# Layer-norm sums through a constant block, four instead of eight units on the un-normed residual, and a reordered last norm

## The chip, the cores and the metric

The kernel runs on one core of a Trainium2 chip. The metric is device time in microseconds (us). The core has a TensorE (in the profile PE for its matmuls and PEld for its weight loads), a VectorE (DVE), a ScalarE (ACT), a GpSimd (POOL) and a SyncE (SP, which here issues nearly all DMAs). Each engine works through its own instruction queue in the order in which the program puts instructions there, and waits on semaphores for the others.

## The reference

A two-layer decoder trunk over 256 tokens with 2048 channels, all float32. Each layer is a mixer, a layer norm, a gated feed-forward net with a causal convolution of width 3, and a second layer norm. Layer 0 mixes by causal pooling, layer 1 by dilated attention.

```
for i in range(DEPTH):                      # 2
    mix = pool_mixer(h, ...)   or   dilated_attention(h, k_shared, v_shared, ...)
    h = layer_norm(ALPHA * h + mix, ln1_g[i], ln1_b[i])
    ff = (silu(conv(h @ gate half)) * conv(h @ value half)) @ w_down
    h = layer_norm(ALPHA * h + ff, ln2_g[i], ln2_b[i])
```

`layer_norm` takes mean and variance over the 2048 channels of a token. K and V are computed once, from the stream after layer 0. Three of the four norms feed matrix products (after the pooling mixer, after the first feed-forward net, after attention); the fourth is the output.

## The kernel before, in words

The stream is kept with channels on the partitions: four quads `H[0..3]`, each 128 partitions by 4 blocks by 256 tokens. All weights (380 MB) are read once from HBM. The work is a list of **units**. A unit is one weight block of 512 rows by (mostly) 512 columns, and four units in a row, one per quad of the input, make a **group**, whose sums stay in four PSUM banks. `run_units` (L96) walks the list: for unit i, `ahead(i)` (L81) puts the load of unit i+5 on SP and the split of unit i+3 into a high part `wh` (a cast on ACT, L76) and a low part `wl` (a subtraction on DVE, L77) into the queues; then come the unit's matmuls, then the functions whose turn it is. `later(n, fn)` (L90) asks that `fn` be emitted after n more units. Nothing is reordered afterwards, so this emission order is the order of each engine's queue. Only four pairs `wh`/`wl` exist, so a cast for unit i+3 waits until TensorE is done with unit i-1.

`mm_quad` (L120) has three modes. For each of 16 blocks (4 row blocks by 4 column blocks), mode "ab" does two products: `wh` against the high and low parts of the input side by side (512 columns, L135), and `wl` against the high part (256 columns, L136). Mode "x" does three products of 258 columns (L138 to L140): the two further columns carry the norm's gain and bias through the weights.

Mode "x" is for the first units behind a norm. The input of such a unit, `XP[q]`, is the residual before the norm times the gain (`xp`, L319); the norm is put in afterwards when the group leaves PSUM (`norm_evac`, L380). So TensorE goes on while the norm's sums are made. Before the change two whole groups behind each of the three inner norms, eight units, are in mode "x": gate and value of the first feed-forward block (`up`, L570), or K and Q of the first four heads (L767 to L770).

Meanwhile the norm itself is made. `resid_last` (L243) adds the last group to `H[3]`, `folds` (L283) leaves in `S` and `Q` the sum and the sum of squares over 16 channel blocks (128 partitions by 256 tokens each), and `chain` (L329) is emitted two units later. It sums over partitions with four products of `S` and `Q` against a column of 1/2048, which leaves the result with tokens on partitions; works out mean and 1/deviation on slivers of 128x2; makes diagonal blocks of them (L345); and one unit later `spread` (L349) copies them to all partitions by four products. Then quad by quad, one unit apart: `norm` (L355, two DVE passes), `affine` (L359, ACT) and `lo` (L367, DVE) make `XC[q]`, the input of all later units.

The last norm is done with tokens on partitions (`tm_post`, L609). The last group of the program does token half 0 first, then half 1 in two column halves. `finish0` (L639) norms half 0: on ACT scale and shift, on DVE times gain (L650) and plus bias (L651), four blocks, and four stores. Three multiplications of half 1 by the gain follow (L632), then the sums of half 1 are added and `finish1` (L655) ends the program with four more stores.

Of the kernel before, what the change touches and what calls it, by code (L numbers as in the profile page):

```python
# [9 lines left out]
F32 = mybir.dt.float32  # L10
# [6 lines left out]
D = 2048  # L17
T = 256
# [14 lines left out]
def trunk(ctx: ExitStack, tc: tile.TileContext, x, pool_w_in, pool_w_grp, pool_scale, pool_w_out,  # L33
# [181 lines left out]
    ones = const.tile([P, 1], F32, name="ones")  # L215
# [27 lines left out]
    def resid_last(c, first, lay, which, after):  # L243
        def post(ps):
            for m in range(4):
                y = H[c][:, m, :]
                if first and c == 0:
                    V.scalar_tensor_tensor(y, y, ALPHA, ps[m][:, :T], op0=OP.mult, op1=OP.add)
                else:
                    V.tensor_tensor(y, y, ps[m][:, :T], OP.add)  # L250
                if c < 3:
                    V.tensor_tensor(y, y, ps[m][:, T:], OP.add)
                if c == 3 and m % 2 == 1:
                    square(3, m - 1)
            if c == 0:
                s = fold(H[0], None, "S0", F32R)
                later(1, lambda: shift(s, first, lay, which))
            elif c < 3:
                n = 3 if c == 1 and not first else 1
                later(n, lambda: stats(c))  # L260
                later(n + 1, lambda: xp(c, lay, which))
            else:
                folds(3)
                xp(3, lay, which)
                later(2, lambda: chain(ps[0], lay, which, after))
        return post

    def square(q, m):
# [50 lines left out]
    def xp(q, lay, which):  # L319
# [6 lines left out]
                                   op0=OP.mult, op1=OP.subtract)  # L326
        A.copy(t[:, :, :, T:], gbx[lay, which][:, 4 * q:4 * q + 4].bitcast(F32))

    def chain(ps, lay, which, after):  # L329
        sm = lnp.tile([P, 16], F32, name="sm", tag="sm")  # L330
        for t in range(2):
            PE.matmul(ps[:, t:t + 1], ST["S"][:, t * P:t * P + P], ones[:, 0:1], start=True, stop=True)
            PE.matmul(ps[:, 2 + t:3 + t], ST["Q"][:, t * P:t * P + P], ones[:, 0:1], start=True, stop=True)
        A.copy(sm[:, 0:4], ps[:, 0:4])
        A.activation(sm[:, 4:6], sm[:, 0:2], AF.Square)
        V.tensor_tensor(sm[:, 6:8], sm[:, 2:4], sm[:, 4:6], OP.subtract)
        A.activation(sm[:, 8:10], sm[:, 6:8], AF.Sqrt, bias=epst)
        V.reciprocal(sm[:, 10:12], sm[:, 8:10])
        V.tensor_tensor(sm[:, 12:14], sm[:, 0:2], sm[:, 10:12], OP.mult)
        dg = lnp.tile([P, 4, P], F32, name="dg", tag="fold2")  # L340
        rm = lnp.tile([P, 4, T], F32, name="rm", tag="sq")[:, 0:2]
        rs, mr = rm[:, 0:1, :], rm[:, 1:2, :]
        ST["rs"], ST["mr"] = rm[:, 0, :], rm[:, 1, :]
        for i in range(4):
            A.activation(dg[:, i, :], ident, AF.Copy, scale=sm[:, 10 + i:11 + i])  # L345
        mb, rb = mr.to_broadcast([P, 4, T]), rs.to_broadcast([P, 4, T])
        g0 = 32 * which

        def spread():  # L349
            for i in range(4):  # L350
                PE.matmul(ps[:, i * P:i * P + P], one1, dg[:, i, :], start=True, stop=True)
            A.copy(rm.rearrange("p a t -> p (a t)"), ps)
            norm(0)

        def norm(q):  # L355
            V.tensor_tensor(H[q], H[q], rb, OP.mult)
            V.tensor_tensor(H[q], H[q], mb, OP.subtract)

        def affine(q):  # L359
            XC[q] = quad_tile("xc")  # L360
            for m in range(4):
                j = 4 * q + m
                A.activation(H[q][:, m, :], H[q][:, m, :], AF.Identity,
                             scale=vec[lay][:, g0 + j:g0 + j + 1], bias=vec[lay][:, g0 + 16 + j:g0 + 17 + j])
            A.copy(XC[q][:, :, 0, :T], H[q])

        def lo(q):  # L367
            lo_part(XC[q], H[q], 4)
            if after is not None:
                later((10, 10, 12, 12)[q], lambda: after(q))  # L370

        later(1, spread)
        for q in range(4):
            later(2 + q, lambda q=q: affine(q))
            if q < 3:
                later(2 + q, lambda q=q: norm(q + 1))
            later(3 + q, lambda q=q: lo(q))


    def norm_evac(ps, nb, tmp, dst):  # L380
# [112 lines left out]
    def ffn(lay):  # L493
# [36 lines left out]

        def gate_post(q, nb, mode):
            def post(ps):
                u = evac(ps, nb, mode)
# [12 lines left out]
                later(1, two)  # L546
            return post

        def val_post(q, nb, mode):
            def post(ps):  # L550
# [19 lines left out]
        def up(q):  # L570
# [2 lines left out]
            mode = "x" if x0 else "ab"  # L573
            group(w_up, rows4, 512 * q, nb * P, psrcs if x0 else xsrcs, gate_post(q, nb, mode),
                  mode=mode)
            group(w_up, rows4, FF + 512 * q, nb * P, psrcs if x0 else xsrcs, val_post(q, nb, mode),
                  mode=mode)

        def down(qs, last=False):
            rows = [(512 * q, min(512, FF - 512 * q)) for q in qs]  # L580
# [28 lines left out]
    def tm_post(c, last):  # L609
        def post(t, ps, half=None):  # L610
# [12 lines left out]
            if c == 2 and t == 1:  # L623
                for nm, w in (("g", ln2_g), ("b", ln2_b)):
                    r = rawp.tile([P, 4, 512], F32, name=nm, tag="raw")
                    nc.sync.dma_start(r.rearrange("p a c -> p (a c)"), w[1:2, :].to_broadcast([P, D]))
                    ST[nm] = r
            if c == 3 and t == 0:
                finish0()
                for cc in range(3):  # L630
                    z = HT[cc][:, 1, :]
                    V.tensor_tensor(z, z, ST["g"][:, cc, :], OP.mult)  # L632
            if c == 3 and half == 1:
                finish1()

        def store(cc, t):
            nc.sync.dma_start(out[0, t * P:(t + 1) * P, 512 * cc:512 * cc + 512], HT[cc][:, t, :])

        def finish0():  # L639
            mv = lnp.tile([P, 6], F32, name="mv", tag="mv", bufs=2)  # L640
# [7 lines left out]
            for cc in range(4):  # L648
                z = HT[cc][:, 0, :]
                V.tensor_tensor(z, z, ST["g"][:, cc, :], OP.mult)  # L650
                V.tensor_tensor(z, z, ST["b"][:, cc, :], OP.add)  # L651
                store(cc, 0)


# [39 lines left out]

    def qk_post(nm, hq):
        def post(ps):
            ap = pools["attn"]
            o = ap.tile([P, 4, T], F32, name=nm, tag=nm)
            qk[nm] = o
# [1 line left out]
            def tmp():  # L701
                return ap.tile([P, T], F32, name="qt", tag="t1", bufs=2)

            if hq == 0:
                norm_evac(ps, 4, tmp, lambda m: o[:, m, :])
            else:
                for m in range(4):
# [70 lines left out]
    with tc.tile_pool(name="start", bufs=1) as stp:  # L778
        for q in range(NQ):
# [12 lines left out]
            if q == 0:  # L792
# [120 lines left out]
```

## Time and profile before

| | us |
|---|---|
| median of three runs | 2081.78 |
| lowest, highest | 2081.38, 2082.88 |
| the profiled execution | 2083.26 |
| its span (first to last instruction) | 2081.1 |
| TensorE busy in the span | 2063.6 (99%) |
| VectorE busy | 1419.9 (68%) |
| ScalarE busy | 1027.3 (49%) |
| mean granted TensorE clock | 0.996 of full speed |

A matmul's end in the profile is modelled and neighbours overlap, so the cost of a matmul in a stream is read from the distance between starts, not from its duration. Starts in the listing are us from the start of the span. Lines such as L138 are lines of the kernel before; the same code stands some lines higher in the changed kernel.

### The profile page before, as it was taken

The numbers are of one execution on the slowest core, as the hardware profiler recorded it, in microseconds if no ns is written. First come the engines' busy times: TensorE is split into PE (matmuls) and PEld (weight loads), VectorE is DVE, ScalarE is ACT, GpSimd is POOL, SyncE is SP. The second block draws the span as 40 slices with busy tenths as digits, with TensorE's granted clock in tenths as the row PEclk, the third lists the DMA queues.
The fourth block names the chain that finished last, engine by engine and source line by source line (L and its number), as shares of the span: only waits on it lengthen the run. The fifth ranks groups of instructions, "written<-read, shape, count | busy, mean of one in ns | idle before, by whom it ended". The sixth has DMA issues, their size and how long they took to land.

```text
span 2081.1 us, 28758 instructions
## 1 busy us (share of the span) xinstructions
PE 2063.6 (99%) x12028; PEld 1815.5 (87%) x12028; DVE 1419.9 (68%) x1783; ACT 1027.3 (49%) x1142; POOL 11.4 (1%) x38
## 2 busy tenths in 40 slices
PE   9999999999999999999999999999999999999997
PEld 8889988888888888889888888998888888888886
DVE  6858787756756766778755667687656664665676
ACT  5545665345534535556544444475535543544552
POOL 2000000000000000000000000000000000000000
PEclk9999999999999999999999999999999999999998
DMA  8655465655565565555555455546555555555463
GB/s 253 216 188 189 155 203 182 202 183 186 178 202 183 182 202 173 187 188 162 182 172 175 163 172 176 194 145 203 192 189 183 185 198 183 183 195 188 153 202 131
DMA packets 195297, 383.98 MB, mean 185 GB/s; under 512 B 7022, under 2 KB 15876, under 8 KB 194912
## 3 DMA queue, kind: packets, MB, share of 16 engines
q1 hardware_dynamic: 194240, 381.71, 56.2%
q8 instruction: 94, 1.54, 0.3%
q0 software_dynamic: 928, 0.44, 0.1%
q14 instruction: 35, 0.29, 0.0%
HBM read 380.01 MB, written 2.10 MB: 184 GB/s over the span
## 4 chain that ended last, share of the span: by engine, by line
PE 98%; DVE 1%; DMA 0%; SPq 0%; ACT 0%; issue 0%
PE acc L135 46%; PE acc L136 23%; PE t L165 5%; PE t L167 5%; PE t L166 5%; PE acc L139 4%; PE acc L138 4%; PE acc L140 4%; DMA xin<-in_x_dram 0%; PE s L722 0%; PE o L762 0%; PE pT L749 0%; PE o L763 0%; PE s L721 0%; PE xT L461 0%; PE hT L605 0%
## 5 line engine op out<-in xcount | busy, mean ns | idle before, releaser
L77 DVE TENSOR_TENSOR wl<-raw,wh 128x2048 fp32r<-128x2048 f32 (+2 forms) x376 | 821.3, 2187 | 508.6 <-ACT wh L76 496.7
L135 PE MATMUL acc<-xc,wh 128*128 128x512 f32 x3072 | 1082.2, 396 | 0.0
L76 ACT CAST wh<-raw 128x2048 fp32r<-128x2048 f32 (+2 forms) x376 | 685.8, 1828 | 600.3 <-PE acc L135 358.2
L136 PE MATMUL acc<-xc,wl 128*128 128x256 f32 x3072 | 862.5, 281 | 0.0
L135 PEld LDWEIGHTS acc<-xc,wh 128*128 128x128 f32 x3072 | 579.9, 189 | 136.0
L136 PEld LDWEIGHTS acc<-xc,wl 128*128 128x128 f32 x3072 | 579.5, 189 | 0.2
L135 PE MATMUL acc<-g,wh 128*128 128x512 f32 x644 | 226.8, 396 | 0.0
L136 PE MATMUL acc<-g,wl 128*128 128x256 f32 x644 | 180.7, 281 | 0.0
L135 PEld LDWEIGHTS acc<-g,wh 128*128 128x128 f32 x644 | 121.6, 189 | 28.3
L527 DVE SCALAR_TENSOR_TENSOR c<-u,cv,c 128x256 f32<-128x256 f32 x344 | 141.8, 478 | 0.7
L165 PE MATMUL t<-wh,g 128*128 128x512 f32 (+1 forms) x355 | 137.9, 389 | 0.0
L166 PE MATMUL t<-wl,g 128*128 128x512 f32 (+1 forms) x355 | 137.4, 387 | 0.0
L167 PE MATMUL t<-wh,g 128*128 128x512 f32 (+1 forms) x355 | 137.3, 387 | 0.0
L136 PEld LDWEIGHTS acc<-g,wl 128*128 128x128 f32 x644 | 121.7, 189 | 0.0
L139 PE MATMUL acc<-xp,wh 128*128 128x258 f32 x384 | 109.2, 284 | 0.0
L138 PE MATMUL acc<-xp,wh 128*128 128x258 f32 x384 | 109.0, 284 | 0.0
L140 PE MATMUL acc<-xp,wl 128*128 128x258 f32 x384 | 108.0, 281 | 0.0
L514 ACT COPY ut<-acc 128x256 f32<-128x256 f32 x156 | 56.6, 373 | 98.6 <-PE acc L136 98.4
L523 ACT ACTIVATE c<-u,cv 128x256 f32<-128x256 f32 x172 | 89.7, 598 | 0.0
L515 DVE TENSOR_TENSOR u<-acc,ut 128x256 f32<-128x256 f32 x156 | 58.2, 416 | 37.5 <-ACT ut L514 37.5
L167 PEld LDWEIGHTS t<-wh,g 128*128 128x128 f32 x355 | 66.7, 188 | 15.1
L165 PEld LDWEIGHTS t<-wh,g 128*128 128x128 f32 x355 | 66.7, 188 | 14.8
(212 smaller groups left out, 2114.4 us busy)
## 6 DMA issues: line engine op xcount, KB each, us to landing
raw<-in_ffn_w_up_dram SPq DMA_DIRECT2D x160, 1024.0 KB, 5.1
raw<-in_ffn_w_down_dram SPq DMA_DIRECT2D x80, 1024.0 KB, 5.1
raw<-in_pool_w_out_dram SPq DMA_DIRECT2D x16, 1024.0 KB, 5.0
raw<-in_shared_w_k_dram SPq DMA_DIRECT2D x16, 1024.0 KB, 5.1
raw<-in_attn_w_q_dram SPq DMA_DIRECT2D x16, 1024.0 KB, 5.1
raw<-in_shared_w_v_dram SPq DMA_DIRECT2D x16, 1024.0 KB, 5.1
raw<-in_attn_w_o_dram SPq DMA_DIRECT2D x16, 1024.0 KB, 5.0
raw<-in_pool_w_in_dram SPq DMA_DIRECT2D x12, 1024.0 KB, 5.5
```

The source lines that it names most:

```text
L76: A.copy(wh[i][:, s], r[:, s])
L77: V.tensor_tensor(wl[i][:, s], r[:, s], wh[i][:, s].bitcast(F32), OP.subtract)
L135: PE.matmul(ps[m], h[:, k, c], q[:, k, :, :T], start=st, stop=False)
L136: PE.matmul(ps[m][:, :T], l[:, k, c], q[:, k, 0, :T], start=False, stop=sp and not shifted)
L138: PE.matmul(ps[m][:, :n], h[:, k, c], q[:, k, 0, :n], start=st, stop=False)
L139: PE.matmul(ps[m][:, :n], h[:, k, c], q[:, k, 1, :n], start=False, stop=False)
L140: PE.matmul(ps[m][:, :n], l[:, k, c], q[:, k, 0, :n], start=False, stop=sp and not shifted)
L165: PE.matmul(to, xh, h[:, k, c], start=j == 0 and k == 0, stop=False)
L166: PE.matmul(to, xh, l[:, k, c], start=False, stop=False)
L167: PE.matmul(to, xl, h[:, k, c], start=False, stop=j == len(r0s) - 1 and k == nk - 1)
L523: A.activation(c[:, m, :], u[:, m, 2:], AF.Identity, scale=cv[:, 2, j:j + 1], bias=cv[:, 3, j:j + 1])
L527: V.scalar_tensor_tensor(c[:, m, :], u[:, m, i:i + T], cv[:, i, j:j + 1], c[:, m, :], op0=OP.mult, op1=OP.add)
```

## The change

Four edits.

1. `chain` multiplies `S` and `Q` (256 columns each) by a constant 128x128 block of 1/2048, so each partition gets every token's mean and mean square at once. The arithmetic on them is now 128x256 wide. `spread`, the diagonal blocks and the slivers are gone. `chain` is emitted one unit, not two, behind the last group, and `norm(0)` is emitted with it.
2. The second "x" group behind each inner norm (value, or Q) becomes an "ab" group on `XC`. The first one (gate, or K) is evacuated two units later than before.
3. In the last norm the three multiplications of half 1 by the gain are emitted two units behind the third group, ahead of `finish0`.
4. In `finish0` the bias is added by a DMA from the POOL queue that accumulates into the block, in place of a DVE addition; the store waits for that DMA.

```
-                later(2, lambda: chain(ps[0], lay, which, after))
+                later(1, lambda: chain(ps[0], lay, which, after))
...
+        PE.matmul(ps[:, :T], onesd, ST["S"], start=True, stop=True)
+        PE.matmul(ps[:, T:], onesd, ST["Q"], start=True, stop=True)
+        rm = lnp.tile([P, 4, T], F32, name="rm", tag="sq")
+        rs, mr, var = rm[:, 0, :], rm[:, 1, :], rm[:, 2, :]
+        ST["rs"], ST["mr"] = rs, mr
+        A.activation(rm[:, 3, :], ps[:, :T], AF.Square)
+        V.tensor_tensor(var, ps[:, T:], rm[:, 3, :], OP.subtract)
+        A.activation(var, var, AF.Sqrt, bias=epst)
+        V.reciprocal(rs, var)
+        V.tensor_tensor(mr, ps[:, :T], rs, OP.mult)
...
-        later(1, spread)
+        norm(0)
         for q in range(4):
-            later(2 + q, lambda q=q: affine(q))
+            if q > 0:
+                later(1 + q, lambda q=q: lo(q - 1))
+            later(1 + q, lambda q=q: affine(q))
             if q < 3:
-                later(2 + q, lambda q=q: norm(q + 1))
-            later(3 + q, lambda q=q: lo(q))
+                later(1 + q, lambda q=q: norm(q + 1))
+        later(5, lambda: lo(3))
...
+                later(2 if mode == "x" else 0, lambda: gate_chain(q, nb, mode, ps))
...
-            group(w_up, rows4, FF + 512 * q, nb * P, psrcs if x0 else xsrcs, val_post(q, nb, mode),
-                  mode=mode)
+            group(w_up, rows4, FF + 512 * q, nb * P, xsrcs, val_post(q, nb, "ab"))
...
+                later(2, early)
             if c == 3 and t == 0:
                 finish0()
-                for cc in range(3):
-                    z = HT[cc][:, 1, :]
-                    V.tensor_tensor(z, z, ST["g"][:, cc, :], OP.mult)
...
+        def early():
+            for cc in range(3):
+                z = HT[cc][:, 1, :]
+                V.tensor_tensor(z, z, ST["g"][:, cc, :], OP.mult)
...
-                V.tensor_tensor(z, z, ST["b"][:, cc, :], OP.add)
+                nc.gpsimd.dma_start(z, ST["b"][:, cc, :], accum_op=OP.add)
                 store(cc, 0)
...
+            later(2 if hq == 0 and nm == "k" else 0, lambda: evac(ps))
...
-            if hq == 0:
+            if hq == 0 and nm == "k":
                 norm_evac(ps, 4, tmp, lambda m: o[:, m, :])
...
-        group(attn_w_q[0], rows4, 512 * hq, 512, psrcs if x0 else xsrcs, qk_post("q", hq), mode="x" if x0 else "ab")
+        group(attn_w_q[0], rows4, 512 * hq, 512, xsrcs, qk_post("q", hq))
...
-        V.memset(ones, 1.0 / D)
+        V.memset(onesd, 1.0 / D)
```

More of the change, by code (lines that the diff above doesn't have):

```diff
@@ L214, in trunk @@
     ident = const.tile([P, P], F32, name="ident")
-    ones = const.tile([P, 1], F32, name="ones")
+    onesd = const.tile([P, P], F32, name="onesd")
     one1 = const.tile([P, P], F32, name="one1")
@@ L329, in chain @@
     def chain(ps, lay, which, after):
[L330 to L346, printed above, removed]
-        g0 = 32 * which
[L349 to L353, printed above, removed]
+        PE.matmul(ps[:, :T], onesd, ST["S"], start=True, stop=True)
[8 more added lines that the diff above has]
+        V.tensor_tensor(mr, ps[:, :T], rs, OP.mult)
+        mb, rb = rm[:, 1:2, :].to_broadcast([P, 4, T]), rm[:, 0:1, :].to_broadcast([P, 4, T])
+        g0 = 32 * which
         def norm(q):
@@ L532, in post, with gate_chain @@
             def post(ps):
+                later(2 if mode == "x" else 0, lambda: gate_chain(q, nb, mode, ps))
+            return post
+        def gate_chain(q, nb, mode, ps):
                 u = evac(ps, nb, mode)
@@ L546, in post @@
                 later(1, two)
-            return post
         def val_post(q, nb, mode):
@@ L696, in post, with evac @@
         def post(ps):
+            later(2 if hq == 0 and nm == "k" else 0, lambda: evac(ps))
+        def evac(ps):
             ap = pools["attn"]
```

## The prediction

> **What bounds the kernel now.** I read the page's busy line and the chain that ended last, then TensorE's listing behind a norm, then the queues that feed it there, then the end of the program. Page, parts 1 and 4:
>
> ```profile
> PE 2063.6 (99%) x12028; PEld 1815.5 (87%) x12028; DVE 1419.9 (68%) x1783; ACT 1027.3 (49%) x1142; POOL 11.4 (1%) x38
> PE 98%; DVE 1%; DMA 0%; SPq 0%; ACT 0%; issue 0%
> ```
>
> TensorE sets the time from the first matmul to the last; the 1% of DVE in the chain is the end of the program. An edit can therefore pay in two ways: TensorE work that goes away counts in full as long as TensorE doesn't wait instead, and the end behind the last matmul counts in full on DVE.
>
> **TensorE behind a norm.** I call the three places A (after pooling), B (after the first feed-forward net), C (after attention). Listing of PE in A, and two other stretches:
>
> ```profile
> 218.02 0.28 PE L138 MATMUL acc<-xp,wh 128*128 128x258 f32 x1
> ...
> 229.57 0.28 PE L332 MATMUL acc<-ones,S 128*128 128x1 f32 x2
> ...
> 230.38 0.37 PE L138 MATMUL acc<-xp,wh 128*128 128x258 f32 x1
> ...
> 236.24 1.06 PE L351 MATMUL acc<-dg,one 128*128 128x128 f32 x8
> 237.05 0.36 PE L138 MATMUL acc<-xp,wh 128*128 128x258 f32 x1
> ...
> 265.88 0.40 PE L135 MATMUL acc<-xc,wh 128*128 128x512 f32 x1
> ...
> 1385.03 0.39 PE L135 MATMUL acc<-xc,wh 128*128 128x512 f32 x1
> ...
> 1424.38 0.49 PE L605 MATMUL hT<-ident,h 128*128 128x128 f32 x3
> ```
>
> Two "x" units take 229.57 - 218.02 = 11.55 us, 5.77 each. The unit from 230.38 to 236.24 takes 5.86, so 0.09 is lost in getting back into step after inserted products. The five units from 237.05 to 265.88 take 28.83; less 0.09 that is 5.75 each. From 1385.03 to 1424.38 stand seven "ab" units, 39.35, so 5.62 each. An "ab" unit is 0.13 us shorter.
>
> *Edit 2 on TensorE.* Four units behind each of three norms change mode: 12 x 0.13 = 1.55 us saved.
>
> *Edit 1 on TensorE.* Before, the sums cost 230.38 - 229.57 = 0.81 and the spreading 237.05 - 236.24 = 0.81, each with 0.09 behind it: 1.8 us per norm. The new products are plain float32 with 256 columns. Such products stand in attention; each is two records:
>
> ```profile
> 1007.24 0.60 PE L722 MATMUL s<-k,q 128*128 128x256 f32 x2
> 1007.67 0.38 PE L721 MATMUL s<-k,q 128*128 128x128 f32 x2
> ```
>
> One costs 0.43; two and one restart cost 0.95. Saved per norm 0.85, for three 2.55. TensorE saves 1.55 + 2.55 = 4.1 us, if `XC[q]` is there when the second group asks for it.
>
> **Is XC there in time?** B is the tightest, so I work it out there. TensorE's clock after the change: K's units from 947.95, plus 0.95 for the sums, so Q's four units want XC[0..3] at 947.95 + 4 x 5.76 + 0.95 = 971.9, then 977.6, 983.2 and 988.8. Rows of before, DVE and ACT in B, then three of A:
>
> ```profile
> 947.95 0.29 PE L138 MATMUL acc<-xp,wh 128*128 128x258 f32 x1
> ...
> 953.54 0.43 DVE L280 TENSOR_TENSOR Q<-Q 128x256 f32<-128x256 f32 x1
> 953.88 1.67 DVE L325 SCALAR_TENSOR_TENSOR xp<-h,vec,xp 128x256 fp32r<-128x256 f32 x4
> 955.46 4.48 DVE L77 TENSOR_TENSOR wl<-raw,wh 128x2048 fp32r<-128x2048 f32 x2
> ...
> 983.04 1.22 DVE L202 TENSOR_TENSOR xc<-h,xc 128x1024 fp32r<-128x1024 f32 x1
> 984.18 1.22 DVE L356 TENSOR_TENSOR h<-h,rm 128x1024 f32<-128x1024 f32 x1
> ...
> 988.77 1.22 DVE L202 TENSOR_TENSOR xc<-h,xc 128x1024 fp32r<-128x1024 f32 x1
> ```
> ```profile
> 953.06 3.72 ACT L76 CAST wh<-raw 128x2048 fp32r<-128x2048 f32 x2
> ...
> 986.69 2.08 ACT L363 ACTIVATE h<-h,vec 128x256 f32<-128x256 f32 x4 [1.02 <-DVE h L357]
> ...
> 989.76 1.91 ACT L76 CAST wh<-raw 128x2048 fp32r<-128x2048 f32 x1
> ```
> ```profile
> 223.31 2.28 DVE L77 TENSOR_TENSOR wl<-raw,wh 128x2048 fp32r<-128x2048 f32 x1
> ...
> 252.84 1.22 DVE L202 TENSOR_TENSOR xc<-h,xc 128x1024 fp32r<-128x1024 f32 x1
> ...
> 261.74 1.22 DVE L202 TENSOR_TENSOR xc<-h,xc 128x1024 fp32r<-128x1024 f32 x1
> ```
>
> Start to start, a `wl` takes DVE 2.2, a `lo` (L202) 1.14, a `norm`, two passes like L356, 2.4; on ACT a cast takes 1.8, `affine` with its copy 3.06. The changed queues, in their order. TensorE reaches the sums at 953.7; `Q` was ready at 953.97, and its product comes second, at 954.1: no wait, by a hair. ACT squares behind one cast (955.0) and loads its table meanwhile. DVE does one `wl` from 955.46, so the variance starts at 957.7 and ends at 958.1; square root 958.6 (0.5, one of the four in L363), reciprocal 959.05, product 959.5, `norm(0)` 961.95. Then DVE: `wl` 964.15, `norm(1)` 966.55. ACT: `affine(0)` and copy 965.1, cast 967.0. DVE: `wl` 969.3, `lo(0)` 970.5. XC[0] is 1.4 us early. From here DVE repeats `norm`, `wl`, `lo`, 5.74 per quad (the rows from 983.04 to 988.77 show 5.73), while TensorE asks every 5.62: XC[1] at 976.2, XC[2] at 982.0, XC[3] at 987.1, early by 1.4, 1.2 and 1.7. ACT needs 4.9 per quad and keeps up. The weight splits stay over 5 us ahead of their units. K's evacuation, now behind `lo(3)`, takes until about 991; its banks are wanted at 994.4. In A the variance starts 223.31 + 2.2 - 218.02 = 7.5 us into the stage, in B 9.7: A has 2.2 us more in hand, and C queues as A does. So I cost the loss on TensorE at nothing; the cover is 1.2 us in B and 3.4 in A and C.
>
> The unknown is the reciprocal on 256 columns. The nearest rows have 1 and 2:
>
> ```profile
> L338 DVE RECIPROCAL sm<-sm 128x2 f32<-128x2 f32 x3 | 0.5, 165 | 4.3 <-ACT sm L337 4.3
> L336 DVE TENSOR_TENSOR sm<-sm 128x2 f32<-128x2 f32 x3 | 0.5, 160 | 6.6 <-ACT sm L335 6.6
> L663 DVE RECIPROCAL mv<-mv 128x1 f32<-128x1 f32 x1 | 0.2, 157 | 0.0
> ```
>
> At most 8 ns come with the second column, so 256 cost at most 0.157 + 255 x 0.008 = 2.2 us; at least what L280 takes on 256, 0.43. The two-column one is only 5 ns above the two-column subtraction (L336), so I take 0.43. The Trainium skill, "VectorE: DVE Perf Modes", section "First, the fixed hardware budget", says that a reciprocal is an iterative divide with a repeat count of 8; my estimate from it and its 0.96 GHz is 2.1 us, and the forecast would be 2074.5.
>
> **The end of the program.** Listing of DVE, ACT and PE:
>
> ```profile
> 2059.24 0.69 DVE L614 TENSOR_TENSOR ht<-ht,t 128x512 f32<-128x512 f32 x1 [5.81 <-PE t L167]
> ...
> 2061.88 2.94 ACT L647 ACTIVATE ht<-ht,mv 128x512 f32<-128x512 f32 x4 [0.42 <-DVE mv L644]
> 2062.73 0.69 DVE L650 TENSOR_TENSOR ht<-ht,g 128x512 f32<-128x512 f32 x1 [0.89 <-ACT ht L647]
> 2063.45 0.69 DVE L651 TENSOR_TENSOR ht<-ht,b 128x512 f32<-128x512 f32 x1
> ...
> 2068.04 1.89 DVE L632 TENSOR_TENSOR ht<-ht,g 128x512 f32<-128x512 f32 x3
> ...
> 2070.64 0.40 DVE L616 TENSOR_TENSOR ht<-ht,t 128x256 f32<-128x256 f32 x1
> ...
> 2077.22 0.75 DVE L671 SCALAR_TENSOR_TENSOR ht<-ht,mv,b 128x512 f32<-128x512 f32 x1
> ```
> ```profile
> 2066.71 0.28 PE L167 MATMUL t<-wh,g 128*128 128x256 f32 x1
> ```
>
> The last matmul ends at 2066.99; the DVE sum that needs it (the second L616) starts only at 2070.64, because DVE is busy without a gap. Edit 3 takes L632's 1.89 out, edit 4 four L651. The four L650 are then paced by ACT: its last of four ends at 2064.82, so L650 ends at 2065.5; the first L616 and its statistics end by 2066.4. Then DVE waits for TensorE, and the second L616 starts at 2067.0: 3.65 us earlier, and with it all that follows. No more can be won here, as TensorE is next. The early multiplications lie in the 5.81 us in which DVE waited ahead of 2059.24.
>
> What edit 4 puts in place: four POOL DMAs of 256 KB, and SP's four half-0 stores behind them, ahead of the half-1 stores on the same queue. The latter are ready at 2074.4 - 3.65 = 2070.8 up to 2077.97 - 3.65 = 2074.3. No accumulating DMA is in the trace; the nearest rows, first two from the list of DMA issues with their us to landing, then what an issue takes POOL and SP:
>
> ```profile
> out_dram<-ht SPq DMA_DIRECT2D x8, 256.0 KB, 2.0
> crow<-in_ffn_conv_w_dram POOLq DMA_DIRECT2D x2, 129.0 KB, 11.8
> ```
> ```profile
> L828 POOL DMA_DIRECT2D crow<-in_ffn_conv_b_dram x2 | 1.1, 551 | 0.0
> ```
> ```profile
> L637 SPq DMA_DIRECT2D out_dram<-ht x8: 332/332/348, 2064.2 to 2078.0; - x8
> ```
>
> So 2.0 to 11.8 us to land. The slow ones ran while the weights streamed in; at the end all loads are done, so I take 2 to 5: POOL issues the last behind L650 by 2066.1, it has landed by 2071, four stores gone before the last is wanted at 2074.3. Cost nothing. The larger `onesd` fill falls into DVE's wait for the input at the start.
>
> **The sum.** 1.55 + 2.55 + 3.65 = 7.75 us. Against the profiled execution, 2083.26: 2075.5. That run is 1.5 above the median; against the median, 2081.78, I predict **2074.0**.
>
> **Rivals.**
> - *The reciprocal is at its upper end.* 1.8 us later in B, 1.2 covered: 0.5 to 0.6 lost once, 2074.5. For it: nothing excludes 8 ns a column. Against: the 5 ns.
> - *The accumulating DMAs are late.* From a landing after about 2073 SP is the bound. If POOL could issue only once DVE's work ends (2074.3): four issues of 0.55, 2 us of landing, five stores at 0.33 to 0.35 and 2 us more end near 2082.2, against some 2080.3 before; 3.65 won turns into 1.9 lost: 2079.6. The Trainium skill, "SBUF — State Buffer", section "SBUF: two separate sides", lets DVE lock GpSimd out of writing DMA descriptors during some instructions; no run here shows it.
> - *Slower: the quads come too slowly.* In A before, `lo` of two quads stand 261.74 - 252.84 = 8.9 us apart, because convolution work lies between. At a spacing p the fourth quad is late by 3 x (p - 5.62) less the cover; over the three stages 9 x (p - 5.62) - 8. At 8.9 that is 21.5 us: 2095.5. It makes the kernel slower beyond the bound from p = 7.8. Against: in the changed queue nothing stands between but `wl`, as in B.
> - *No gain at the end, or half-hidden stalls of 4 us or so:* 2078.
>
> **How the numbers follow.** Forecast 0.66; reciprocal 0.12; late DMAs 0.10, half of it inside 0.2% (4.2 us, about what can be told from no change); too slow quads 0.07; the last 0.05. Faster 0.66 + 0.12 + 0.05 = 0.83, same 0.10, slower 0.07. Range: down to 2072.8, a little over 1 us for sums that are exact only to a few hundredths per unit, up to 2078.0, which leaves out the slow quads and half of the late DMAs.
>
> **What would show it.** The products on `onesd` take about 0.9 us and Q's first unit follows K's last without a gap; PE idle stays near nothing; the second L616 starts within 0.1 us of the last matmul's end; SP's last store is issued right behind DVE's end. A gap in PE ahead of Q's or value's units, or stores bunched behind the POOL DMAs, would prove me wrong.

## The result, and the profile after

| | before | after |
|---|---|---|
| median, us | 2081.58 | 2074.39 |
| lowest, highest | 2081.10, 2082.88 | 2073.05, 2074.48 |
| profiled execution | 2083.26 | 2074.43 |
| its span | 2081.14 | 2072.65 |

The changed kernel is faster: ratio 0.9964, 95% interval 0.9954 to 0.9974. The prediction, 2074.0, is 0.4 us off.

The busy line and the chain that ended last of the changed kernel:

```profile
PE 2058.3 (99%) x11800; PEld 1801.5 (87%) x11800; DVE 1420.3 (69%) x1767; ACT 1019.7 (49%) x1112; POOL 14.9 (1%) x42
PE 99%; DVE 0%; DMA 0%; SPq 0%; ACT 0%; issue 0%
```

TensorE still sets the time. The listing of PE in A, then in B, where the units of Q follow K's four:

```profile
216.38 0.28 PE L138 MATMUL acc<-xp,wh 128*128 128x258 f32 x1
...
222.16 0.60 PE L331 MATMUL acc<-S,onesd 128*128 128x256 f32 x2
222.60 0.59 PE L332 MATMUL acc<-Q,onesd 128*128 128x256 f32 x2
222.84 0.47 PE L138 MATMUL acc<-xp,wh 128*128 128x258 f32 x1
...
240.29 0.40 PE L135 MATMUL acc<-xc,wh 128*128 128x512 f32 x1
...
944.86 0.29 PE L138 MATMUL acc<-xp,wh 128*128 128x258 f32 x1
...
968.81 0.47 PE L135 MATMUL acc<-xc,wh 128*128 128x512 f32 x1
...
974.54 0.47 PE L135 MATMUL acc<-xc,wh 128*128 128x512 f32 x1
...
980.27 0.47 PE L135 MATMUL acc<-xc,wh 128*128 128x512 f32 x1
...
985.98 0.40 PE L135 MATMUL acc<-xc,wh 128*128 128x512 f32 x1
...
991.65 0.40 PE L165 MATMUL t<-wh,xc 128*128 128x512 f32 x1
```

The two products take 222.84 - 222.16 = 0.68 us, and the first "ab" unit follows the last "x" product without a gap. Yet Q's four units in B take 991.65 - 968.81 = 22.84 us, 0.36 more than four times 5.62. Why is in DVE's listing of the same stretch and in the group of the reciprocal:

```profile
955.58 1.75 DVE L339 RECIPROCAL rm<-rm 128x256 f32<-128x256 f32 x1 [0.58 <-ACT rm L338]
...
967.44 1.22 DVE L202 TENSOR_TENSOR xc<-h,xc 128x1024 fp32r<-128x1024 f32 x1
...
973.17 1.22 DVE L202 TENSOR_TENSOR xc<-h,xc 128x1024 fp32r<-128x1024 f32 x1
...
984.03 1.22 DVE L202 TENSOR_TENSOR xc<-h,xc 128x1024 fp32r<-128x1024 f32 x1
```
```profile
L339 DVE RECIPROCAL rm<-rm 128x256 f32<-128x256 f32 x3 | 5.3, 1754 | 2.9 <-ACT rm L338 2.9
```

`XC[0]` is ready at 967.44 + 1.22 = 968.66, 0.15 us ahead of its unit, and `XC[1]` at 974.39, again 0.15 ahead. These 0.15 us are no cover: in `recip_x3` below, where TensorE certainly waits for `XC[0]`, its unit starts 0.14 us behind the end of `lo`. So TensorE here takes each of the first three quads as soon as DVE delivers it. The second and the third unit start 974.54 - 968.81 = 5.73 and 980.27 - 974.54 = 5.73 us behind the one before, which is DVE's time for a quad; the third takes 985.98 - 980.27 = 5.71, as its first product needs 0.32 us to the next start in place of 0.23.

Four fixed points make the runs comparable: the first unit of A, of B and of C, and the start of the last down group of the program (I call what lies from there to the end of the span the last part). The distances between them leave out the first microseconds, in which TensorE waits for the input's DMAs and which differ from run to run.

| us | before | after | difference |
|---|---|---|---|
| start to A | 218.02 | 216.38 | -1.64 |
| A to B | 729.93 | 728.48 | -1.45 |
| B to C | 389.08 | 387.89 | -1.19 |
| C to the last part | 668.37 | 666.78 | -1.59 |
| the last part | 75.74 | 73.12 | -2.62 |

The 1.64 is no effect of the change: other kernels below with the same code up to A start it anywhere from 215.65 to 218.67. That would also account for the profiled execution of before, 1.5 above its median; the executions without a profile don't show where they started. The change itself gives 4.23 us on TensorE and 2.62 at the end.

The end of the changed kernel, listings of DVE, PE and SP's and POOL's issues, then its list of DMA issues (KB each, us to landing):

```profile
2059.59 0.42 DVE L609 TENSOR_TENSOR ht<-ht,t 128x256 f32<-128x256 f32 x1
...
2061.16 0.42 DVE L609 TENSOR_TENSOR ht<-ht,t 128x256 f32<-128x256 f32 x1 [0.69 <-PE t L167]
...
2067.76 0.75 DVE L667 SCALAR_TENSOR_TENSOR ht<-ht,mv,b 128x512 f32<-128x512 f32 x1
...
2060.84 0.28 PE L167 MATMUL t<-wh,g 128*128 128x256 f32 x1
...
2061.22 7.65 SPq L628 DMA_DIRECT2D out_dram<-ht  x8
...
2057.86 3.58 POOL L647 DMA_DIRECT2D ht<-b  x4 [1659.01 <-DVE ht L646]
```
```profile
out_dram<-ht SPq DMA_DIRECT2D x8, 256.0 KB, 2.7
ht<-b POOLq DMA_DIRECT2D x4, 256.0 KB, 4.4
```

The second half sum (L609) starts at 2061.16, right behind the last matmul's end at 2061.12. DVE ends at 2068.51, 7.39 us behind the last matmul; before it was 10.98. That is 3.59 won. But the span ends 4.14 us behind DVE, where it was 3.17 before: 0.97 is given back.

### The profile page after: what moved, and what is told of

Its sections match the earlier page's. It is cut to its first block, busy times and chain, and to the rows that moved or that the text cites. A ratio compares the mean times of both kernels' runs of the same rounds, so it can differ in the third digit from the quotient of the medians.

```text
span 2072.7 us, 28276 instructions
## 1 busy us (share of the span) xinstructions
PE 2058.3 (99%) x11800; PEld 1801.5 (87%) x11800; DVE 1420.3 (69%) x1767; ACT 1019.7 (49%) x1112; POOL 14.9 (1%) x42
## 3 DMA queue, kind: packets, MB, share of 16 engines
q8 instruction: 92, 1.51, 0.3%
## 4 chain that ended last, share of the span: by engine, by line
PE 99%; DVE 0%; DMA 0%; SPq 0%; ACT 0%; issue 0%
PE acc L135 48%; PE acc L136 25%; PE t L165 5%; PE t L167 5%; PE t L166 5%; PE acc L139 3%; PE acc L140 3%; PE acc L138 3%; PE s L721 0%; PE o L761 0%; DMA raw<-in_pool_w_in_dram 0%; PE pT L748 0%; PE o L762 0%; PE s L720 0%; PE hT L598 0%; DVE ht L667 0%
## 5 line engine op out<-in xcount | busy, mean ns | idle before, releaser
L135 PE MATMUL acc<-xc,wh 128*128 128x512 f32 x3264 | 1150.0, 396 | 0.0
L136 PE MATMUL acc<-xc,wl 128*128 128x256 f32 x3264 | 916.2, 281 | 0.0
L135 PEld LDWEIGHTS acc<-xc,wh 128*128 128x128 f32 x3264 | 616.3, 189 | 144.9 <-issue 0.2
L136 PEld LDWEIGHTS acc<-xc,wl 128*128 128x128 f32 x3264 | 615.7, 189 | 0.2
L166 PEld LDWEIGHTS t<-wl,g 128*128 128x128 f32 x355 | 66.8, 188 | 14.4
L135 PE MATMUL acc<-o,wh 128*128 128x512 f32 x192 | 67.9, 397 | 0.0
L135 PE MATMUL acc<-mixed,wh 128*128 128x512 f32 x192 | 67.5, 395 | 0.0
```

Of the source, the lines that this page charges most:

```text
L135: PE.matmul(ps[m], h[:, k, c], q[:, k, :, :T], start=st, stop=False)
L136: PE.matmul(ps[m][:, :T], l[:, k, c], q[:, k, 0, :T], start=False, stop=sp and not shifted)
L166: PE.matmul(to, xh, l[:, k, c], start=False, stop=False)
```

## The experiments

Theory: TensorE saves about 4.1 us as summed; the end saves about 3.6 on DVE and loses part of it to the four accumulating DMAs; all holds only while the quads reach TensorE in time. Rivals: the gain of the end is DVE's alone and something else lengthens the stores; the cover behind the norms is wide; the place of the evacuations does not matter.

**The two halves apart.** `norms_only` keeps edits 1 and 2; `tail_only` keeps edits 3 and 4 and has everything else as before.

```
 norms_only:                       # edits 3 and 4 undone
-                later(2, early)
             if c == 3 and t == 0:
                 finish0()
+                for cc in range(3):
+                    z = HT[cc][:, 1, :]
+                    V.tensor_tensor(z, z, ST["g"][:, cc, :], OP.mult)
...
-                nc.gpsimd.dma_start(z, ST["b"][:, cc, :], accum_op=OP.add)
+                V.tensor_tensor(z, z, ST["b"][:, cc, :], OP.add)
 tail_only:                        # edits 1 and 2 undone
-                later(1, lambda: chain(ps[0], lay, which, after))
+                later(2, lambda: chain(ps[0], lay, which, after))
...
-            group(w_up, rows4, FF + 512 * q, nb * P, xsrcs, val_post(q, nb, "ab"))
+            group(w_up, rows4, FF + 512 * q, nb * P, psrcs if x0 else xsrcs, val_post(q, nb, mode),
+                  mode=mode)
...
```

> Edits 1 and 2 alone, the end of the program as before. My theory (TensorE's saving counts in full, the end is a separate account): 4.2 us less than the kernel before, as the starts in A, B and C moved by 1.45, 1.12 and 1.58 us in the changed kernel; the end of the program as long as before. Rival (part of the 7.2 us is luck in the first 15 us of the program, which began 1.6 us earlier in the changed kernel's profile): A, B and C still give 4.2, whatever the start does, and the start differs from run to run.

Measured: 2076.98 against 2081.54, 4.56 us faster (ratio 0.9981, interval 0.9971 to 0.9990). By the distances between the fixed points it is 4.26, and the last part takes 75.76 us, as before.

> Edits 3 and 4 alone. Theory (DVE's end comes 3.6 us earlier, but the accumulating DMAs keep all 16 DMA engines full from 2061 on, and the last store lands about 1 us later for it): 2.5 us less than before. Rival (the late landing in the changed kernel's profile was chance): 3.6 us less.

Measured: 2078.69 against 2081.54, 2.85 us faster (0.9986, 0.9977 to 0.9995). The two add up to 7.41, as much as the whole change (7.2). The interval of `tail_only` covers -2.5 as well as -3.6, so the times don't decide between its theory and the rival. Its profile does: the last part takes 72.79 us, 2.95 less than before, with DVE's end 3.60 earlier and 0.65 given back behind it. No interaction needs explaining.

**What edit 4 costs and what it wins.** Three kernels change only the one line of the bias in half 0. `dve_bias` lets DVE add it again, `pool_add` lets GpSimd add it, and `no_bias0` leaves it out.

```
                 V.tensor_tensor(z, z, ST["g"][:, cc, :], OP.mult)
-                nc.gpsimd.dma_start(z, ST["b"][:, cc, :], accum_op=OP.add)
+                V.tensor_tensor(z, z, ST["b"][:, cc, :], OP.add)          # dve_bias
+                nc.gpsimd.tensor_tensor(z, z, ST["b"][:, cc, :], OP.add)  # pool_add
                 store(cc, 0)                                              # no_bias0: neither
```

> The changed kernel with edit 4 undone: the bias of half 0 is added by DVE again. Theory: DVE's end is 1.8 us later than in the changed kernel, the last store lands 1 us sooner after its issue, so 0.7 to 0.8 us slower than the changed kernel. Rival (the accumulating DMAs cost nothing): 1.8 us slower than the changed kernel.

> The bias of half 0 added by a GpSimd addition in place of the accumulating DMA. Theory (the accumulating DMAs fill the DMA engines and delay the last store by 1 us): DVE's end as in the changed kernel, the last store lands 2.0 us behind its issue, 1 us faster than the changed kernel, if GpSimd takes no more than 1.5 us per block. Rival (DVE and GpSimd get in each other's way in SBUF): DVE's instructions at the end get longer and the end comes later than in the changed kernel.

> The changed kernel without the bias of half 0 in the last norm (the four accumulating DMAs are left out and nothing takes their place, so half 0 of the output lacks its bias). It prices edit 4's DMAs by themselves, since DVE's order stays as it is. My theory: DVE's work behind the last matmul ends as before (some 68.9 to 69.0 us after the start of the program's last part), but the four half-0 stores go out with DVE's multiplications, are gone when those of half 1 come, land in about 2.0 us each, and the time from DVE's end to the program's end falls back from 4.2 to the 3.1 us of the kernel before: 1.06 us less in the program's last part (72.1 in place of 73.17). Rival: what grew to 4.2 us is the last store by itself, ending later for another reason than the accumulating DMAs: less than 0.3 us gained. The kernel with three accumulating DMAs got 0.64 of it back (72.53), so a value between 72.4 and 72.6 would say that the fourth DMA alone did the harm.

Measured: `dve_bias` 2075.15 (ratio to before 0.9969, 0.9957 to 0.9982), `pool_add` 2074.77 (0.9971, 0.9959 to 0.9982), `no_bias0` 2073.55 (0.9959, 0.9945 to 0.9973). The medians differ by less than the intervals, so I read the last part in the profiles, us from its start:

| | DVE ends | from there to the end | in it: issue to landing of the last store | in it: from that landing to the end | last part |
|---|---|---|---|---|---|
| before | 72.57 | 3.17 | 1.98 | 1.15 | 75.74 |
| after | 68.98 | 4.14 | 2.60 | 1.51 | 73.12 |
| tail_only (same end) | 68.97 | 3.82 | 2.28 | 1.51 | 72.79 |
| dve_bias | 70.76 | 3.19 | 2.01 | 1.15 | 73.95 |
| pool_add | 70.30 | 3.55 | 2.00 | 1.52 | 73.85 |
| no_bias0 | 68.97 | 3.19 | 2.00 | 1.15 | 72.16 |

In `before`, `dve_bias` and `no_bias0` the end behind DVE is 3.17 to 3.19 us; with four accumulating DMAs it is 3.82 and 4.14. So they cost 0.6 to 1.0 us, as the theory of `no_bias0` had it, and against DVE's addition (1.78 later) edit 4 wins only 0.8 to 1.2. The cost has two parts. The last store lands 0.3 to 0.6 us later, and 0.36 more passes between its landing and the end. The second part is not the DMA engines' doing: `pool_add`, which has no accumulating DMA, shows it too. It stands in every run here in which POOL works in the last part (1.51 to 1.53 us) and in none in which it doesn't (1.14 to 1.15); what fills it no run here shows. (The 73.17, 72.53 and 1.06 of the expectations come from spans rounded to a tenth.)

How the first part comes about stands in the windows of the end. The columns are the stretch and its length, the busy time of PE, PEld, DVE, ACT and POOL, the granted clock, the DMA engines' busy share and GB/s. First after, then before (the same place behind DVE), then `no_bias0`:

```profile
2058.00:2061.00 3.00, 3.00 (x27) 2.91 (x25) 2.40 (x5) 0.95 (x2) 2.94 (x4) 1.00 0.57 96
2061.00:2064.00 3.00, 0.12 (x2) 0.00 (x0) 2.71 (x6) 0.29 (x1) 0.43 (x1) 1.00 1.10 185
2064.00:2067.00 3.00, 0.00 (x0) 0.00 (x0) 2.93 (x6) 0.00 (x0) 0.00 (x0) 0.66 1.06 311
2067.00:2070.00 3.00, 0.00 (x0) 0.00 (x0) 1.47 (x3) 0.00 (x0) 0.00 (x0) 0.50 1.01 374
```
```profile
2073.00:2076.00 3.00, 0.00 (x0) 0.00 (x0) 2.90 (x7) 0.00 (x0) 0.00 (x0) 0.50 0.24 92
2076.00:2079.00 3.00, 0.00 (x0) 0.00 (x0) 1.94 (x3) 0.00 (x0) 0.00 (x0) 0.50 0.49 190
```
```profile
2064.00:2067.00 3.00, 0.00 (x0) 0.00 (x0) 2.93 (x5) 0.00 (x0) 0.00 (x0) 0.50 0.47 175
2067.00:2070.00 3.00, 0.00 (x0) 0.00 (x0) 0.75 (x1) 0.00 (x0) 0.00 (x0) 0.50 0.47 175
```

After the change all DMA engines are busy for 9 us, because half-0 stores wait for the accumulating DMAs and then fall together with half 1's: the eight stores are issued between 2061.2 and 2068.5, in `no_bias0` between 2056.8 and 2067.8. In `no_bias0` no transfer is left between 2061 and 2064 and the share behind is 0.47; each store lands in 2.0 us, as before, in place of a median of 2.7:

```profile
out_dram<-ht SPq DMA_DIRECT2D x8, 256.0 KB, 2.0
```

`pool_add` keeps the stores short too, but the rows of its addition and of the multiplications beside it, against those of the changed kernel, show another price:

```profile
L647 POOL TENSOR_TENSOR ht<-ht,b 128x512 f32<-128x512 f32 x4 | 6.4, 1621 | 1658.7 <-DVE ht L646 1658.7
...
2056.40 4.80 DVE L646 TENSOR_TENSOR ht<-ht,g 128x512 f32<-128x512 f32 x4 [0.89 <-ACT ht L643]
```
```profile
2056.86 2.82 DVE L646 TENSOR_TENSOR ht<-ht,g 128x512 f32<-128x512 f32 x4 [0.88 <-ACT ht L643]
```

DVE's four multiplications take 4.80 us beside GpSimd in place of 2.82, and DVE ends 1.3 us later, as the rival of this run had it. The Trainium skill, "SBUF — State Buffer", section "Who interferes with whom", says that a DVE instruction with two inputs in SBUF contends with a GpSimd instruction that reads SBUF; this run agrees.

`mix` uses what this showed. The last block has its bias added by DVE, in DVE's wait of 0.69 us for the last matmul, and only three DMAs accumulate.

```
+                if cc == 3:
+                    V.tensor_tensor(z, z, ST["b"][:, cc, :], OP.add)
+                else:
+                    nc.gpsimd.dma_start(z, ST["b"][:, cc, :], accum_op=OP.add)
```

> The changed kernel, but the last of the four blocks of half 0 gets its bias by a DVE addition again, blocks 0 to 2 by the accumulating DMAs. My theory: the addition (0.69 us) lies in DVE's wait for the last matmul and costs DVE's end nothing; the POOL queue issues one DMA fewer (1.0 us), the half-0 stores are gone about 1 us sooner and the DMA engines hold 256 KB less of accumulating traffic when the half-1 stores start, so that of the 1.06 us between DVE's end and the program's end which edit 4 gave back 0.3 to 0.6 come back: 0.3 to 0.6 us faster than the changed kernel, ratio to the kernel before 0.996 or just under. Rival: the time behind DVE's end is set by the stores of half 1 alone or by the other three accumulating DMAs: no difference from the changed kernel (within 0.2 us). Rival on the other side: DVE's addition delays the first sum of half 1 and the statistics behind it: 0.3 to 0.7 us slower.

Measured: 2074.08 (2073.71 to 2074.10), ratio 0.9961, 0.9947 to 0.9975. Its listing and DMA list:

```profile
2059.94 0.69 DVE L648 TENSOR_TENSOR ht<-ht,b 128x512 f32<-128x512 f32 x1
...
2067.99 0.75 DVE L670 SCALAR_TENSOR_TENSOR ht<-ht,mv,b 128x512 f32<-128x512 f32 x1
```
```profile
ht<-b POOLq DMA_DIRECT2D x3, 256.0 KB, 3.9
```

DVE ends 68.97 us into the last part, so the addition is free, and the rest is 3.57: the last store lands in 2.01 us again, and 1.53 follow its landing, as in every run that uses POOL late. The last part is 72.54, 0.25 to 0.58 shorter than with four DMAs. The median is 0.3 lower than the changed kernel's. Both agree with the expectation, but 0.3 us is not told apart by these runs; `mix` is the best version here by its profile, not by a proven difference.

**How wide is the cover behind the norms?** `recip_x3` makes two more reciprocals, 3.5 us on DVE in the chain; `cheap_recip` puts a product of 0.43 us in the reciprocal's place.

```
         V.reciprocal(rs, var)
+        V.reciprocal(var, rs)                   # recip_x3
+        V.reciprocal(rs, var)
...
-        V.reciprocal(rs, var)
+        V.tensor_tensor(rs, var, var, OP.mult)  # cheap_recip
```

> Two more reciprocals on 128x256 behind the first (there and back, the values stay), 3.5 us more in the path of each norm. Theory (XC is 0.15 us early in B, 1.5 us early in A and C): gaps of 3.4 us in B and 2.0 us in A and C, and a granted clock of about 0.5 for some microseconds behind a gap, as behind the gaps of 4 to 6 us in the run with the evacuation not delayed: 7.4 us slower without the drop, up to 12 with it behind all three. Rival (the reciprocal is off the path): no gap.

Measured: 2084.86 (one run), 10.5 above the changed kernel. TensorE waits 1.97 us in A, 3.57 in B and 1.94 in C ahead of the first "ab" unit, 7.48 in all, against 2.0, 3.4 and 2.0 expected. I count a wait from start to start less the 0.12 of one product; the listing, with its modelled ends, gives a little less. So the cover that was left after the change is 1.5 us in A and C and nothing in B. The three distances between the fixed points grow by 3.60, 4.86 and 2.25, 10.71 together. Of the 3.23 beyond the waits 2.9 come from the clock in A and B (last section). The 0.3 in C, where the clock stayed at 1.00, is DVE's pace: its first three "ab" units take 5.73, 5.74 and 5.69 us. B's wait in the listing of PE, behind the `lo` of DVE that ends it:

```profile
974.34 1.22 DVE L202 TENSOR_TENSOR xc<-h,xc 128x1024 fp32r<-128x1024 f32 x1
...
975.70 0.48 PE L135 MATMUL acc<-xc,wh 128*128 128x512 f32 x1 [3.41 <-DVE xc L202]
```

A and C are not 2.2 us ahead of B, as forecast, but 1.6 (in the changed kernel `XC[0]` is ready 22.17 us into A and 23.80 into B), because there the table of the square root is loaded in the path: DVE waits 1.18 us in A and 1.16 in C for the square root, in B 0.58. ACT and DVE in A of the changed kernel:

```profile
223.63 1.28 ACT L338 ACT_TABLE_LOAD   x1
...
225.47 1.75 DVE L339 RECIPROCAL rm<-rm 128x256 f32<-128x256 f32 x1 [1.18 <-ACT rm L338]
```

> The reciprocal replaced by a product of the same size (0.42 us in place of 1.75), so the norm's values are not the reference's. Theory (the reciprocal's length is what lets DVE set the pace of the second group in B): Q's four units in B take 22.5 us in place of 22.84, A and C the same, 0.3 us faster in all. Rival (DVE's 5.73 us per quad sets the pace whatever the reciprocal takes): 22.8 as before.

Measured: 2073.64 (one run). A to B is 728.48, as after; C to the last part 666.79, as after to 0.01; B to C 387.56, 0.33 less. Q's four units in B take 22.53 in place of 22.84. So the long reciprocal costs 0.3 us, once, in B.

**The order of the work behind the norm.** `gate_now` takes out the two units by which gate and K are evacuated later; nothing else changes.

```
-                later(2 if mode == "x" else 0, lambda: gate_chain(q, nb, mode, ps))
+                later(0, lambda: gate_chain(q, nb, mode, ps))
...
-            later(2 if hq == 0 and nm == "k" else 0, lambda: evac(ps))
+            later(0, lambda: evac(ps))
```

> The changed kernel with the two-unit delay of the first group's evacuation taken out, so some 3 us of DVE work stand between the second and the third quad's low part. Theory (in the changed kernel XC is 1.5 us early in A and C and 0.15 us early in B): TensorE stalls 1.4 us in A and in C and 2.9 us in B, about 5.7 us slower than the changed kernel. Rival (the cover is larger than I read it): less than 1 us slower.

Measured: 2096.12 (one run), 21.7 above the changed kernel and far beyond the 5.7 expected. Waits of PE (total, times, longest), and DVE's listing in B:

```profile
PE acc L135 <- ACT c L514: 7.8, 2, 3.9
PE acc L135 <- DVE xc L202: 5.7, 1, 5.7
```
```profile
981.04 1.22 DVE L202 TENSOR_TENSOR xc<-h,xc 128x1024 fp32r<-128x1024 f32 x1
...
987.11 0.87 DVE L380 SCALAR_TENSOR_TENSOR qt<-rm,wgb,qt 128x256 f32<-128x256 f32 x2
990.41 2.29 DVE L77 TENSOR_TENSOR wl<-raw,wh 128x2048 fp32r<-128x2048 f32 x1 [2.43 <-ACT wh L76]
992.62 1.22 DVE L202 TENSOR_TENSOR xc<-h,xc 128x1024 fp32r<-128x1024 f32 x1
```

The list names ACT for two of the waits, but all three end 0.14 to 0.15 us behind the `lo` of the quad that the unit needs, so it is `lo` that TensorE waits for. The second and the third `lo` are 992.62 - 981.04 = 11.6 us apart in place of 5.73: the evacuation's passes stand between, and DVE also waits 2.43 for a cast that queues behind the evacuation's ACT work. That is 5.9 us more; the 2.9 expected for the evacuation was half of it. The gaps are 4.06, 5.86 and 4.03 us; the three distances grow by 5.70, 8.15 and 5.65, so another 5.5 us are lost behind the gaps, again to the clock; A also starts 2.17 later, which is no effect of the edit. This is the rival "the quads come too slowly", made real for one quad in each stage: the two units' delay is worth some 20 us.

**Are four "x" units possible without the constant block?** `old_sums` goes back to the column products, the narrow arithmetic and `spread` one unit later. `old_sums2` is the same, with the evacuation three units later rather than two.

```
 both:
-        PE.matmul(ps[:, :T], onesd, ST["S"], start=True, stop=True)
-        PE.matmul(ps[:, T:], onesd, ST["Q"], start=True, stop=True)
...
+        for t in range(2):
+            PE.matmul(ps[:, t:t + 1], ST["S"][:, t * P:t * P + P], ones[:, 0:1], start=True, stop=True)
+            PE.matmul(ps[:, 2 + t:3 + t], ST["Q"][:, t * P:t * P + P], ones[:, 0:1], start=True, stop=True)
...
-        norm(0)
+        later(1, spread)
...
 old_sums2 also:
-                later(2 if mode == "x" else 0, lambda: gate_chain(q, nb, mode, ps))
+                later(3 if mode == "x" else 0, lambda: gate_chain(q, nb, mode, ps))
...
-            later(2 if hq == 0 and nm == "k" else 0, lambda: evac(ps))
+            later(3 if hq == 0 and nm == "k" else 0, lambda: evac(ps))
```

> The changed kernel with the old way of summing and spreading (products with a column, slivers, diagonal blocks, four spreading products a unit later), still begun one unit sooner. Theory (the block product saves TensorE 0.85 us per norm and, because no second unit has to pass, keeps the norm ahead of the second group): 2.55 us of products come back; by the queues of B XC[0] is then 1.8 us late there and just in time in A and C; 4.4 us slower than the changed kernel. Rival (the sums' form matters to TensorE's work alone): 2.55 us slower, no gap ahead of the second group.

Measured: 2094.66 against 2081.17, slower than the kernel before (1.0065, 1.005 to 1.008) and beyond both expectations. The first gaps are 0.66, 1.78 and 0.53 us, 2.97 in all: B's is as expected, in A and C none was. And a second one stands in each stage, at the fourth quad: 3.08, 3.54 and 3.10. The run mixes two things: with all quads one unit later, the evacuation came ahead of the last `lo`.

> The changed kernel with the old making of the norm's sums (products against a column, arithmetic on 128x2, spreading one unit later), chain still one unit behind the last group, four units in mode x; this time the first group behind the norm is evacuated three units later instead of two, so that its work stands behind the last lo in the queues. Question: is it the constant block alone that lets four units do? My theory: the old way makes XC one unit later (5.6 us less the shorter chain), so Q's or value's first unit waits 0.5 to 0.7 us in A and C and 1.8 us in B, as in the run before with the old sums; the second gaps of that run (3.1 to 3.5 us at the fourth quad) came only from the evacuation standing ahead of the last lo, and are gone. Sum against the changed kernel: products 3 x 0.85 = 2.55, first gaps 3.0, up to 1.5 for a lower granted clock behind B's gap: 5.5 to 7.5 us slower. Rival: the second gaps stay (the delay of XC, not the order of emission, made them): 15 to 20 us slower. Second rival: no gaps at all, 2.5 us slower; then the constant block pays on TensorE alone and four units would have done with the old sums.

Measured: 2081.03 (one run), 6.64 above the changed kernel, inside 5.5 to 7.5, though the granted clock behind B's gap stayed at 1.00. The waits of PE in `old_sums` and then in `old_sums2`:

```profile
PE acc L135 <- DVE xc L202: 11.8, 6, 3.4
```
```profile
PE acc L135 <- DVE xc L202: 2.5, 3, 1.6
```

The second gaps are gone, so order of emission made them; the first stay at 0.66, 1.77 and 0.53. The distances between the fixed points are 730.37, 390.84 and 668.50, against 729.94, 389.07 and 668.36 of `tail_only`, which has the old sums and eight "x" units: 2.34 us more, as the times say too (one run of 2081.03 to a median of 2078.69). Of this 2.96 are gaps, less 1.55 for the shorter units. The other 0.9 is DVE's pace again: the four units behind each gap take 22.80, 22.83 and 22.79 us, where those of `cheap_recip` take 22.47, 22.53 and 22.50. So edit 2 with the old sums, as emitted here, loses; the constant block makes it pay. Edit 1 with eight "x" units was not tried.

## Why the prediction was right, and where its steps were off

- *TensorE behind a norm, 4.1 us.* Right: 4.23, with B's loss in it. Four units at 0.13 and 0.85 for the products make 1.37 a stage; A gave 1.45, C 1.59. The products cost 0.68 with about 0.17 behind them (17.45 us for the three units from 222.84), 0.85 in place of my 0.95.
- *Is XC there in time?* The order and the spacing were right: DVE at 5.73 per quad, units wanted at 5.62, no gap. The mis-sized term is the reciprocal, which I took at 0.43: it measures 1.754, nearer to the upper end of 2.2 that I had worked out from the two-column row than to 0.43. The 5 ns between a one- or two-column reciprocal and a subtraction say little about 256 columns. With the 0.15 us from DVE's end to TensorE's start, which I had not counted, it used up B's cover of 1.4, and TensorE then loses about 0.1 on each of three units: 0.3 us, as `cheap_recip` shows. This is the rival with the reciprocal at its upper end, at 0.3 us in place of its 0.5 to 0.6.
- *Cover in A and C, 3.4 us.* The reciprocal takes 1.33 of it, so 2.1 should be left; `recip_x3` says 1.5. I had the square root's table loaded "meanwhile"; in B it is, but in A and C its load stands in the path and takes some 0.6 more.
- *The end on DVE, 3.65 us.* Right: 3.59. The second L609 starts 0.04 us behind the last matmul's end.
- *"Cost nothing" for the accumulating DMAs.* This step failed. The issue on POOL was put at 0.55 us by the nearest row; the four took 3.58 us of POOL. Their landing, 4.4 us in the middle and 6.1 at the longest, is about the 2 to 5 that I took, and SP's last store is issued right behind DVE's end, as forecast. But the step counted only a queue in which a store waits, and not the DMA engines: they are full from 2061 to 2070, and the last store lands 0.3 to 0.6 us late. The sign that I had named for it, stores bunched behind the POOL DMAs, is there. The other 0.36, between the landing and the end, was in no step. Against `no_bias0` the four DMAs cost 0.96 us in the changed kernel and 0.63 in `tail_only`. The rival of late DMAs, 5.6 us lost, was not met either; the loss was about a sixth of that.
- *Slower, if quads come too slowly.* It did not happen, for the reason given, but it was close at hand: without the later evacuation the kernel takes 2096.1. That this is near the 2095.5 worked out is chance: the rival had every quad come at 8.9 us and no loss to the clock, the run has one gap in each stage, 14.0 us together, 5.5 lost behind the gaps and a start 2.2 later. My price for the place of that evacuation, before `gate_now`, was too small.
- *The sum.* 7.75 was predicted, 7.2 measured by the medians and 6.85 by the two profiles without their starts. The errors are -0.97 behind DVE's end, -0.3 in B, and +0.1 to 0.2 at each of three norms. They are small and partly cancel, and the medians differ by 0.3 more than the distances, which is within their scatter. So that the forecast is only 0.4 us off is in part luck; by the working it is 0.9 off.
- *The chances.* Half of the late DMAs' 0.10 was said to lie outside 0.2%, yet the whole 0.10 went to "same"; faster should have had 0.88. Nothing hangs on it.

## What to carry to other kernels

Where one engine is full, a wide operation on the chain that feeds it is priced by its own duration at that width, not by a narrow row of it: the cover of 1.4 us in B was gone with one reciprocal. When work is moved off an engine onto DMAs, look at the share of the DMA engines in that stretch and not only at the queue, and at everything between the last computation and the end: here the last store landed 0.3 to 0.6 us later, and 0.36 more passed behind it. And a function emitted one unit earlier or later can be worth more than the arithmetic that it does: here the place of the evacuations was worth some 20 us, by one run, the whole change 7.

## What the runs showed of the hardware that I had not expected

*A gap of 2 us can cost as much again.* Behind some gaps of TensorE the granted clock falls to a half for 3 to 4 us. Windows of `recip_x3` around A's gap of 1.97 us, then around C's of 1.94 (the granted clock is the third number from the end):

```profile
240.00:242.00 2.00, 0.19 (x3) 0.05 (x1) 2.00 (x3) 1.97 (x3) 0.00 (x0) 1.00 0.20 22
242.00:244.00 2.00, 2.00 (x7) 1.73 (x8) 1.97 (x2) 1.23 (x1) 0.00 (x0) 0.62 0.87 298
244.00:246.00 2.00, 2.00 (x8) 1.68 (x7) 2.00 (x2) 1.73 (x4) 0.00 (x0) 0.53 0.58 219
246.00:248.00 2.00, 2.00 (x13) 1.78 (x12) 2.00 (x3) 1.97 (x3) 0.00 (x0) 1.00 0.23 22
```
```profile
1366.00:1368.00 2.00, 1.21 (x7) 1.10 (x8) 1.97 (x3) 2.00 (x2) 0.00 (x0) 1.00 0.63 151
1368.00:1370.00 2.00, 2.00 (x13) 1.73 (x12) 2.00 (x2) 0.97 (x3) 0.00 (x0) 1.00 0.96 372
```

The same gap costs 1.63 us more in A (3.60 against 1.97), and in C nothing that the clock shows. The gap of 1.77 in `old_sums2` left the clock at 1.00; those of 3.6 and more (`recip_x3`, `gate_now`) all cost 1.3 to 2.3 on top. Length alone doesn't decide: of the second gaps in `old_sums`, A's of 3.08 us left the clock at 1.00, and behind C's of 3.10 it was at 0.50 for 4 us. The Trainium skill, "TensorE: Matmul & The Clock Gate", section "What's actually happening", has the array fall to half rate after an idle window of about 3.4 us that runs freely, and return after as long a busy one. The 3 to 4 us at the lower clock fit that, and a window that runs freely could explain why equal gaps differ, which no run here tests; but a gap of 1.97 us is shorter than that window and was enough, and here the measurement decides.

*The reciprocal* on 128x256 takes 1.754 us, four times a subtraction of that size (0.42, L337).

*Accumulating DMAs* of 256 KB land in 4.4 us in the middle and take 0.86 to 1.22 us of POOL each (3.58 for the four, which overlap), where a plain store of the same size lands in 2.0.
